# Tiles laid out anew in a partition: moved tiles at its lower end, weights, residual and scratch at its upper end

## The chip, the core and the metric

The kernel runs on one core of a Trainium2 chip. The metric is the time of one execution on the device in microseconds, the median of several. The on-chip memory that the engines work from (SBUF) has 128 partitions; a tile takes the same bytes in each of them, so its place is told by one number, its first byte in a partition. A matmul of TensorE has two operands in that memory: the stationary tile, 128 columns that are loaded into the array ahead of it (a weight load, PEld in the profile), and the moving tile, whose columns (up to 512) are streamed through. The profile names them as out<-moving,stationary.

## The reference

A sequence of 512 tokens of width 1024, in float32, goes through two layers of a first block and one of a second:

```
for l in range(2):
    x = x + 0.5 * swiglu_ffn(x, ffn1...)          # 1024 -> 2816 -> 1024
    h = rms_norm(x, mix_norm[l])
    aq, ak, av, bq, bk, bv, cq, ck, cv, cg, gates = split(h @ w_in[l])
    y_a, y_b, y_c = diff_attention(...), chunk_attention(...), retention(...)
    merged = sum over a, b, c of sigmoid(gates) * (y @ w_branch)
    x = x + merged @ w_out[l]
    x = x + 0.5 * swiglu_ffn(x, ffn2...)
h = rmsnorm(x, norm_mix)                          # second block
q, k, v, z, xbc, dt_raw, g_lru, x_lru = split(h @ w_in_2)
x = x + concat(dilated_attention, ssd_mixer, rglru_mixer) @ w_out_2
x = x + swiglu(rmsnorm(x, norm_ffn), ...)
out = rmsnorm(x, norm_final)
```

## The kernel before

**Numbers in two parts.** Every big product is made of three matmuls in a reduced float32 type (fp32r): both operands are split into a high and a low part (`split_late`: ScalarE writes the high one, VectorE the low one), and `mm3` issues high times high, low times high and high times low into one accumulator. Weights come from memory as a stream of units of 128x1024 (`load`, tile raw, on SyncE's queue), are split into wh and wl (`prepare`), three buffers each, and are used in the order of a fixed plan.

**Products.** Activations lie with features on partitions and the 512 tokens along the row. `fm_tile` makes 128 columns of h @ w: eight steps over k, the weights stationary, xgh[k] and xgl[k] (the normed input's two parts, one tile of 512 columns per k) moving; these are the gate and up products of the feed-forward layers and many of the mixers'. In `ffn` their results become yh and yl, eleven tiles of each for half of the 2816 features; the down products move these, eleven steps for each accumulator. In the mixers, `tm_products` (for q, k, v) is the other way round: xgh and xgl are stationary, and 384 or 512 columns of wh and wl move. The branches' outputs (y; those of branch A in the tiles of x) are moved by the branch products, mh and mb (the merged sum) by w_out, ys, yl and ya by the second block's w_out_2. Small products (scores, p @ v, transposes, sums over partitions) are taken up between the big ones, in an order that the program works out by its own estimates when it is traced. The first product of the second block, for dt, has eight stationary columns for each k, beside each other in one unit of weights.

**Where tiles lie.** Each pool (`Pool`, over a tile pool) is a stretch of the partition; tiles with one tag share its slots. In `Net.__init__` the pools are made one after the other from the lower end: constants; w (raw, wh, wl); x (the residual x in four pairs, xgh and xgl); s (scratch). On top of these come the pools of a stage, which are opened and closed with it: in `ffn` one with g, u, sg, yh and yl; in `mix` and `hybrid` y and mix. `x_pair` gives the memory of two tiles of x; while x is parked in memory, branch A's outputs use it.

The places as the built program has them, in bytes from the start of a partition, with the remainder by 256:

| tiles | before | rem. | after | rem. |
|---|---|---|---|---|
| wh, wl | 33,824 to 58,400 | 32 | 204,768 to 229,344 | 224 |
| x (four pairs) | 58,400 to 74,784 | 32 | 176,096 to 192,480 | 224 |
| xgh, xgl | 74,784 to 107,552 | 32 | 21,760 to 54,528 | 0 |
| diag (two) | 109,600 to 113,696 | 32 | 166,176 to 170,272 | 32 |
| yh, yl | 133,856 to 178,912 | 224 | 54,528 to 99,584 | 0 |
| y, ys, mh, mb | 123,616 to 229,088 | 224 | 54,528 to 164,096 | 0 |
| ones | 20,992 to 21,504 | 0 | the same | 0 |

Of the kernel before, what the change touches and what calls it, by code (L numbers as in the profile page):

```python
# [9 lines left out]
F32 = mybir.dt.float32  # L10
F32R = mybir.dt.float32r
# [5 lines left out]
P = 128  # L17
# [12 lines left out]
# columns of w_in  # L30
# [4 lines left out]
# columns of w_in_2  # L35
# [34 lines left out]
class Uses:  # L70
    """When the regions of a tile are written and read, by the estimate."""
# [17 lines left out]
class Model:  # L89
    """An estimate of when each instruction starts and ends; only the order of issue rests on it."""  # L90
# [4 lines left out]
    def tile(self, ring, bufs, name):  # L95
        """A new tile of a ring of slots."""
        slots = self.rings.setdefault(ring, [])
        if len(slots) < bufs:
            ready = 0.0
        else:  # L100
            old = slots.pop(0)
            ready = self.uses.pop(old).last()
            self.dead.add(old)
        slots.append(name)
        self.uses[name] = Uses(ready)
# [54 lines left out]
class Engine:  # L160
    """An engine's instructions, with an estimate of when each one ends."""
# [46 lines left out]
class Queue:  # L208
    """Transfers issued by an engine, in order."""
# [33 lines left out]
class Later:  # L243
    """The instructions of an engine for a generator: each is issued once it could soon start."""
# [17 lines left out]
class Thread:  # L262
    """A generator that yields the time at which to go on, or a condition."""
# [5 lines left out]
class Net:  # L269
    """Instructions are issued in the order in which they are traced here. The products with the big  # L270
    weights are traced by plain code; the chains of small steps of attention and the like are generators,
    taken up between those products when the estimate says that their operands are there."""
# [7 lines left out]
    def __init__(self, ctx, tc, io):  # L280
        self.tc, self.nc, self.io = tc, tc.nc, io
        self.now, self.last, self.threads, self.accs, self.current, self.seq = 0.0, 0.0, [], [], None, 0
        self.model, self.dma_free = Model(), 0.0
        self.v = Engine(self, self.nc.vector, "v")
        self.a = Engine(self, self.nc.scalar, "a")
        self.tv, self.ta = Later(self.v), Later(self.a)
        self.g = Queue(self, self.nc.gpsimd, "g")
        self.q = Queue(self, self.nc.sync, "q")
        self.aq = Queue(self, self.nc.scalar, "aq")
        self.plan = weight_plan()  # L290
        self.used, self.off, self.at, self.raws, self.splits = 0, 0, {}, [], []
        self.free = {k: [f"{k}_{i}" for i in range(n)] for k, n in self.LIMITS.items()}
        self.banks = set(range(self.BANKS))
        self.n = 0
        pool = lambda name, bufs, **k: self.pool(ctx, name, bufs, **k)
        self.const = pool("const", 1)
        self.wp = pool("w", 3)
        self.xp = pool("x", 1)
        self.sp = pool("s", 2)
        self.pp = pool("ps", 1, space=bass.MemoryType.PSUM)  # L300
        self.dram = pool("dram", 1, space=bass.MemoryType.DRAM)
# [13 lines left out]
    def ready(self):  # L315
        """The thread to go on with: of those that can, the oldest."""
        ok = [t for t in self.threads if (t.wake() if callable(t.wake) else t.wake <= self.now)]
        return min(ok, key=lambda t: t.rank) if ok else None
# [14 lines left out]
    def wait(self, cond):  # L333
        """For plain code."""
# [10 lines left out]
    def take(self, name):  # L345
        """For plain code: one of the slots of that name."""
        self.wait(lambda: self.free[name])
        return self.free[name].pop(0)

    def lock(self, name):  # L350
        """For generators."""
# [12 lines left out]
    def acc(self):  # L364
        """A bank for plain code; it is free when the generator given to evac is done."""
# [11 lines left out]
    def get_bank(self):  # L377
        """For generators: a bank of PSUM that nothing reads any more."""
# [13 lines left out]
    def main_bank(self):  # L392
        """For plain code."""
# [19 lines left out]
    def operands(self, out, ins):  # L413
        """For generators: waits until a product could start."""
# [25 lines left out]
    def load_consts(self):  # L440
# [11 lines left out]
        warm = c.tile([P, 1], F32, name="warm")  # L452
# [27 lines left out]
    def x_pair(self, j, dtype=F32):  # L480
        """The memory of two tiles of x."""
        t = self.xp.tile([P, 2, S], dtype, tag=f"x_{j}", name=self.nm("x"))
# [41 lines left out]
    def tiles(self, units):  # L524
        """128x128 stationary tiles in their order."""
# [24 lines left out]
    def token_rstd(self, sqs, count, eps, n=NT):  # L550
        """Squares [features, tokens] -> 1/rms as [tokens of a tile, tile]."""
# [10 lines left out]
    def spread(self, r, n=NT):  # L562
        """[tokens of a tile, tile] -> the same row of tokens on every partition, in a bank of PSUM: the column
        sums of diagonal blocks, in two parts."""
# [26 lines left out]
    def feed_norm(self, d, gain, feeds):  # L591
        """x[d] is final: its part of the next norm's input and of the sum of squares."""
# [44 lines left out]
    def fm_tile(self, name, l, c0):  # L637
        """128 columns of h @ w (before the norm's factor), features on partitions."""
# [5 lines left out]
    def tm_products(self, name, l, cols, evac):  # L644
        """Some columns of h @ w, tokens on partitions; evac(t, ps) for the tiles of tokens."""
# [16 lines left out]
    def tm_group(self, name, l, cols, nv):  # L662
        """q, k as [token, tile, 256] and v split, with the norm's factor."""
# [30 lines left out]
    def ffn(self, wg, wu, wd, l, factor, gain):  # L694
        self.end_norm()
        with ExitStack() as ctx:
            fp = self.pool(ctx, self.nm("ffn"), 2)
# [6 lines left out]
            def up(ps, got, y, before):  # L704
# [3 lines left out]
                y += [fp.tile([P, S], F32R, tag=t, name=self.nm(t), bufs=HALF) for t in ("yh", "yl")]  # L708
# [29 lines left out]
    def last_products(self, fp, wd, l, ys, factor):  # L738
        """The last products, the norm and the output for one half of the tokens, then for the other."""
# [61 lines left out]
    def rope(self, tm, cos, sin):  # L801
        """cos and sin: for the pairs of heads of q and of k; sin has its signs."""
# [13 lines left out]
    def to_fm(self, tm, c0, tag, scale=None):  # L816
        """128 columns of tm -> [column, token], split."""
# [17 lines left out]
    def scores(self, ps, q, k, i, c):  # L835
        """[query of tile i, key] of one member of the pair, keys up to tile i."""
# [5 lines left out]
    def new_p(self, i):  # L842
        """Probabilities of query tile i for both members, and columns for maxima, sums and their inverses."""
# [3 lines left out]
    def put_pT(self, pT, w, i, *before):  # L847
        """Row block i of a [query, key] matrix into the split [key, key tile, query]."""
# [14 lines left out]
    def new_pT(self):  # L863
        """The visible part of [key, key tile, query]: queries from the key tile's first one."""
# [5 lines left out]
    def av(self, v, pT):  # L870
        """[feature of v, query]"""
# [12 lines left out]
    def out_norm(self, b, o, gain, y, gate=None):  # L884
        """y = o / rms(o) * gain (* gate); o in bank b."""
# [17 lines left out]
    def setup_A(self, l):  # L903
        """-lambda, and cos and sin times the gains of q (with the scale of the scores) and of k."""
# [146 lines left out]
    def rel_rows(self, l, h):  # L1051
        """The biases of a pair of heads, by distance, once per partition."""
# [56 lines left out]
    def fill(self, l, kinds):  # L1109
        """Products for which there is always something to do: p parks tanh(gates / 2) of a tile of the branches  # L1110
        b and c, u parks two tiles of sigmoid(gates) * (y @ w) of branch a, doubled."""
# [43 lines left out]
    def silu_gate(self, l, h, out):  # L1155
        """2 silu(cg) of a head."""
# [13 lines left out]
    def merge(self, l, yb, yc, heads_c):  # L1170
        """sum over the branches of sigmoid(gates) * (y @ w), twice that before the split: the first loads, and a
        function that does the rest."""
# [143 lines left out]
    def softplus(self, v, n):  # L1316
        """max(v, 0) + log1p(exp(-|v|)); the logarithm as 2 atanh(e / (2 + e))."""
# [19 lines left out]
    def lru_scale(self):  # L1337
        """4 softplus(-lambda) and -8 softplus(-lambda)"""
# [11 lines left out]
    def tconv(self, x, out, w, b, j, nj):  # L1350
        """Causal convolution of four taps along the tokens."""
# [7 lines left out]
    def lru_gates(self, j, ps, out):  # L1359
        """The convolution, sigmoid r and sigmoid i times the convolution."""  # L1360
# [23 lines left out]
    def lru_scan(self, parts, scale):  # L1384
        """a = exp(-8 r softplus(-lambda)), and sqrt(1 - a^2) = sqrt(t) (1 + a) with t = tanh(-log(a) / 2)."""
# [68 lines left out]
    def ssd(self, big, xbc, before):  # L1454
        """The scan over chunks of 128 tokens; leaves [feature, token] of each pair of heads, with the skip."""
# [6 lines left out]
        # token-major x (times dt, and times the decay to the chunk's end) and B  # L1462
# [21 lines left out]
        # C B^T per chunk and group: [key, chunk, query]  # L1484
# [11 lines left out]
        # states before each chunk: [state, chunk - 1, head, feature]  # L1496
# [86 lines left out]
    def hybrid(self):  # L1583
        self.end_norm()
        parked = self.park_x()
        with ExitStack() as ctx:
# [5 lines left out]
            # state space: dt, x, B, C  # L1592
# [11 lines left out]
            # recurrence: input and gates  # L1604
# [160 lines left out]
def fm_units(name, l, c0):  # L1765
    """In one transfer, but for the first of all."""
# [194 lines left out]
```

## Time and profile before

| | |
|---|---|
| time, median of 3 runs | 3282.43 us (3281.28 to 3287.72) |
| span of the profiled execution | 3283.1 us |
| TensorE, matmuls | 3264.9 us busy, 15592 |
| TensorE, weight loads | 2721.6 us busy |
| VectorE | 1874.0 us busy |
| ScalarE | 1230.7 us busy |
| moved by DMA | 343.51 MB, 105 GB/s over the span |

The profile is of one execution. Busy time of a group is the union of its instructions' times; a matmul's duration includes its way through the array, so durations of matmuls that follow each other overlap, and their rate is read from their starts. The granted clock of TensorE (PEclk) is given as a share of full speed: 1.00 is 2.4 GHz, 0.50 is 1.2 GHz.

### The profile page before, as it was taken

What the parts mean: (1) busy time and instruction counts of PE and PEld (TensorE: products, weight loads), DVE (VectorE), ACT (ScalarE), POOL (GpSimd) and SP (SyncE); (2) the same over time, 40 slices, a digit from 0 to 9 for tenths busy, and PEclk for the clock granted to TensorE, in tenths of its full rate; (3) what the DMA queues carried; (4) which work ended last, traced back from release to release, by engine and by line L of the source; (5) the groups of instructions that cost most, each with busy time, mean ns of one, the idle gap of its engine ahead of it and who ended that gap; (6) DMA issues with size and microseconds to landing.
All of it is one profiled execution on the core that took longest, in us unless ns stands there. A gap on an engine that the chain in (4) does not pass through costs nothing.

```text
span 3283.1 us, 39855 instructions
## 1 busy us (share of the span) xinstructions
PE 3264.9 (99%) x15592; PEld 2721.6 (83%) x15592; DVE 1874.0 (57%) x3574; ACT 1230.7 (37%) x1996; POOL 111.4 (3%) x206
## 2 busy tenths in 40 slices
PE   9999999999999999999999999999999999999998
PEld 7888888988788888888888888888888788888888
DVE  5434577766754345434478775665344777564345
ACT  4223344653332233222344564333223355642223
POOL 0000000000100000000010000110000000000000
PEclk9999999999999999999999999999999999999999
DMA  4222433223522222222243322342223313222224
GB/s 142 96 97 96 130 107 117 91 83 117 165 95 96 96 96 90 100 95 95 93 137 113 108 84 87 132 151 90 97 97 106 111 66 103 84 86 100 90 98 147
DMA packets 106413, 343.51 MB, mean 105 GB/s; under 512 B 19680, under 2 KB 20864, under 8 KB 106224
## 3 DMA queue, kind: packets, MB, share of 16 engines
q1 hardware_dynamic: 83520, 289.04, 26.5%
q0 software_dynamic: 22704, 51.93, 4.8%
q8 instruction: 122, 2.00, 0.2%
q14 instruction: 67, 0.55, 0.1%
HBM read 319.88 MB, written 26.21 MB: 105 GB/s over the span
## 4 chain that ended last, share of the span: by engine, by line
PE 75%; issue 24%; DVE 1%; DMA 0%; ACT 0%; SPq 0%; POOL 0%; DVEq 0%; POOLq 0%
PE acc L404 66%; PE b L404 7%; PE b L433 2%; DMA rowsA<-in_rows_dram 0%; DMA raw<-in_wst_dram 0%; DVE o L203 0%; DVE rst L203 0%; DVE og L203 0%; DVE rsy L203 0%; SPq L224 0%; DVE mb L203 0%; DVE p L203 0%; DVE y L203 0%; DVE tabA L203 0%; ACT y L203 0%
## 5 line engine op out<-in xcount | busy, mean ns | idle before, releaser
L404 PE MATMUL acc<-xgh,wh 128*128 128x512 f32 x2432 | 959.8, 395 | 1.8 <-ACT xgh L203 1.8
L404 PE MATMUL acc<-xgh,wl 128*128 128x512 f32 x2432 | 950.2, 391 | 0.0
L404 PE MATMUL acc<-xgl,wh 128*128 128x512 f32 x2432 | 949.9, 391 | 0.4 <-DVE xgl L203 0.3
L203 DVE TENSOR_TENSOR wl<-raw,wh 128x1024 fp32r<-128x1024 f32 (+3 forms) x563 | 669.2, 1189 | 470.3 <-ACT wh L203 467.8
L203 ACT CAST wh<-raw 128x1024 fp32r<-128x1024 f32 (+3 forms) x563 | 573.9, 1020 | 872.7 <-issue 444.5
L404 PEld LDWEIGHTS acc<-xgh,wh 128*128 128x128 f32 x2432 | 458.7, 189 | 100.3 <-issue 3.5
L404 PEld LDWEIGHTS acc<-xgh,wl 128*128 128x128 f32 x2432 | 458.2, 188 | 96.6
L404 PEld LDWEIGHTS acc<-xgl,wh 128*128 128x128 f32 x2432 | 458.6, 189 | 94.7 <-DVE xgl L203 1.8
L404 PE MATMUL acc<-yl,wh 128*128 128x512 f32 (+1 forms) x1032 | 382.6, 376 | 0.0
L404 PE MATMUL acc<-yh,wh 128*128 128x512 f32 (+1 forms) x968 | 361.7, 374 | 0.0
L404 PE MATMUL acc<-yh,wl 128*128 128x512 f32 (+1 forms) x968 | 361.5, 373 | 0.0
L404 PE MATMUL acc<-wh,xgh 128*128 128x384 f32 (+1 forms) x672 | 246.9, 367 | 0.0
L404 PE MATMUL acc<-wh,xgl 128*128 128x384 f32 (+1 forms) x672 | 235.4, 350 | 0.0
L404 PE MATMUL acc<-wl,xgh 128*128 128x384 f32 (+1 forms) x672 | 234.9, 350 | 0.0
L203 ACT ACTIVATE sg<-g 128x512 f32<-128x512 f32 x110 | 69.6, 633 | 432.2 <-DVE g L203 432.0
L404 PEld LDWEIGHTS acc<-yl,wh 128*128 128x128 f32 x1032 | 192.4, 187 | 39.7 <-issue 0.5
L404 PEld LDWEIGHTS acc<-yh,wl 128*128 128x128 f32 x968 | 181.8, 188 | 36.6
L404 PEld LDWEIGHTS acc<-yh,wh 128*128 128x128 f32 x968 | 181.2, 187 | 36.6
L203 DVE TENSOR_TENSOR g<-acc,rbc 128x512 f32<-128x512 f32 x110 | 76.1, 691 | 234.9 <-PE acc L404 234.7
L203 DVE TENSOR_TENSOR u<-acc,rbc 128x512 f32<-128x512 f32 x110 | 76.0, 691 | 195.7 <-PE acc L404 195.7
L404 PEld LDWEIGHTS acc<-wh,xgh 128*128 128x128 f32 x672 | 126.9, 189 | 15.7 <-issue 7.4
L404 PEld LDWEIGHTS acc<-wl,xgh 128*128 128x128 f32 x672 | 126.9, 189 | 6.4
(276 smaller groups left out, 3370.7 us busy)
## 6 DMA issues: line engine op xcount, KB each, us to landing
raw<-in_wst_dram SPq DMA_DIRECT2D x496, 512.0 KB, 3.2
raw<-in_wst_dram SPq DMA_DIRECT2D x64, 384.0 KB, 3.4
gpark<-gl POOLq DMA_DIRECT2D x48, 256.0 KB, 3.9
mb<-gpark POOLq DMA_DIRECT2D x48, 256.0 KB, 3.8
xpark<-x POOLq DMA_DIRECT2D x24, 256.0 KB, 5.6
x<-xpark POOLq DMA_DIRECT2D x24, 256.0 KB, 4.8
relscr<-in_rel_dram POOLq DMA_DIRECT2D x8, 639.0 KB, 21.1
bias<-relscr POOLq DMA_DIRECT2D x16, 256.0 KB, 5.1
```

Source lines behind the costliest of these rows:

```text
L203: return f(*a, **k)
L404: self.nc.tensor.matmul(out, lhsT, rhs, start=start, stop=stop)
L433: self.nc.tensor.transpose(out, in_, ident)
```

## The change

Pools can be made from the lower end of the partition (the default) or from the upper end (side="right"). The change makes the pool of xgh and xgl directly after the constants; w, a new pool r for the residual x, and s go to the upper end. The last of the constants, a tile of one column, is given 56 columns more, so that what comes after it starts on a multiple of 256 bytes. In `ffn`, yh and yl get a pool of their own (ffny), made ahead of the one with g, u and sg, so that they come directly after xgl. Nothing is computed in another way; comments and docstrings are gone too, so that lines are shifted by one or two. The order of the instructions on TensorE, VectorE, GpSimd and the queues is the same in the built program, name by name, and so are their waits; on ScalarE six waits are added, at three places.

```diff
         self.const = pool("const", 1)
-        self.wp = pool("w", 3)
         self.xp = pool("x", 1)
-        self.sp = pool("s", 2)
+        self.wp = pool("w", 3, side="right")
+        self.rp = pool("r", 1, side="right")
+        self.sp = pool("s", 2, side="right")
...
-        warm = c.tile([P, 1], F32, name="warm")
+        warm = c.tile([P, 1 + 56], F32, name="warm")[:, 0:1]
...
     def x_pair(self, j, dtype=F32):
-        t = self.xp.tile([P, 2, S], dtype, tag=f"x_{j}", name=self.nm("x"))
+        t = self.rp.tile([P, 2, S], dtype, tag=f"x_{j}", name=self.nm("x"))
...
     def ffn(self, wg, wu, wd, l, factor, gain):
...
+            fy = self.pool(ctx, self.nm("ffny"), HALF)
             fp = self.pool(ctx, self.nm("ffn"), 2)
...
-                y += [fp.tile([P, S], F32R, tag=t, name=self.nm(t), bufs=HALF) for t in ("yh", "yl")]
+                y += [fy.tile([P, S], F32R, tag=t, name=self.nm(t)) for t in ("yh", "yl")]
```

## Rows read from the trace of the kernel before

**Rows 1.** Page, busy us of each engine (share of the span) and instructions.

```profile
PE 3264.9 (99%) x15592; PEld 2721.6 (83%) x15592; DVE 1874.0 (57%) x3574; ACT 1230.7 (37%) x1996; POOL 111.4 (3%) x206
```

**Rows 2.** TensorE's waits, whole run: total us, times, longest us.

```profile
PE b L404 <- DVE rsy L203: 2.4, 1, 2.4
PE acc L404 <- ACT y L203: 1.8, 2, 0.9
```

**Rows 3.** Tile xgh, 3100 to 3210 us: count, durations in ns, first and last start.

```profile
L404 PE MATMUL acc<-xgh,wh x158: 389/389/389, 3100.1 to 3206.9; 128*128 128x512 f32 x158
```

**Rows 4.** Tile yl, 145 to 204 us, a down stretch.

```profile
L404 PE MATMUL acc<-yl,wh x72: 394/394/394, 144.7 to 194.4; 128*128 128x512 f32 x72
```

**Rows 5.** Tile mb, 900 to 937 us, w_out.

```profile
L404 PE MATMUL acc<-mb,wh x39: 393/393/398, 900.0 to 926.6; 128*128 128x512 f32 x39
```

**Rows 6.** Windows: length, TensorE busy (instructions), granted clock, DMA share, GB/s.

```profile
11.70:16.30 4.60, 4.60 (x12) 0.50 1.03 413
```

**Rows 7.** Timeline, first weights: start us, us, what.

```profile
12.08 0.63 PE L404 MATMUL acc<-xgh,wh 128*128 128x512 f32 x1
...
15.92 0.63 PE L404 MATMUL acc<-xgh,wh 128*128 128x512 f32 x1
```

**Rows 8.** Groups by form: shape and count, busy us, mean ns, idle before.

```profile
L404 PE MATMUL acc<-xgh,wh 128*128 128x512 f32 x2432 | 959.8, 395 | 1.8 <-ACT xgh L203 1.8
...
L404 PE MATMUL acc<-yl,wh 128*128 128x512 f32 x856 | 333.1, 395 | 0.0
...
L404 PE MATMUL acc<-wh,xgh 128*128 128x384 f32 x512 | 181.4, 354 | 0.0
...
L404 PE MATMUL acc<-wh,xgh 128*128 128x512 f32 x160 | 65.5, 409 | 0.0
...
L404 PE MATMUL acc<-mh,wh 128*128 128x512 f32 x128 | 50.6, 396 | 0.0
...
L404 PE MATMUL acc<-yh,wh 128*128 128x256 f32 x176 | 49.7, 282 | 0.0
...
L404 PE MATMUL acc<-x,wh 128*128 128x512 f32 x128 | 41.6, 406 | 0.0
```

**Rows 9.** Timeline, branch A's product over x, three matmuls to the next start.

```profile
678.37 0.61 PE L404 MATMUL acc<-x,wh 128*128 128x512 f32 x2
...
679.05 2.03 PE L404 MATMUL b<-pT,v 128*128 128x512 f32 x12
```

**Rows 10.** Timeline, a q, k, v product, twelve matmuls between these starts.

```profile
473.08 0.33 PE L404 MATMUL acc<-wh,xgh 128*128 128x384 f32 x1
...
475.16 0.33 PE L404 MATMUL acc<-wh,xgh 128*128 128x384 f32 x1
```

**Rows 11.** Tile yl, 3225 to 3229 us, the last down products.

```profile
L404 PE MATMUL acc<-yl,wh x12: 281/281/281, 3225.0 to 3228.9; 128*128 128x256 f32 x12
```

**Rows 12.** Timeline, product for dt: matmuls 1, 7 and the next after 18.

```profile
2575.24 0.39 PE L404 MATMUL b<-xgh,wh 128*8 128x512 f32 x1
...
2576.60 0.40 PE L404 MATMUL b<-xgh,wh 128*8 128x512 f32 x1
...
2579.39 0.95 PE L404 MATMUL b<-ones,sq 128*128 128x1 f32 x8
```

**Rows 13.** Timeline, switch from yl, yh to xgh: matmuls 1, 7 and 10.

```profile
194.86 0.39 PE L404 MATMUL acc<-xgh,wh 128*128 128x512 f32 x1
...
196.24 0.39 PE L404 MATMUL acc<-xgh,wh 128*128 128x512 f32 x1
...
196.92 0.39 PE L404 MATMUL acc<-xgh,wh 128*128 128x512 f32 x1
```

**Rows 14.** Timeline, a matmul over diag between those over xgh.

```profile
31.91 0.40 PE L404 MATMUL acc<-xgh,wl 128*128 128x512 f32 x1
32.15 0.39 PE L404 MATMUL b<-diag,ones 128*128 128x512 f32 x1
32.38 0.39 PE L404 MATMUL acc<-xgh,wh 128*128 128x512 f32 x1
```

## Prediction

> **What bounds the kernel now.** I read the page's busy table first: TensorE is busy 3264.9 of 3283.1 us, every other engine far less [rows 1]. Then the waits of TensorE: the longest of them all comes to 2.4 us in total [rows 2]. So nothing feeds TensorE late, and what an edit is worth is read from how fast TensorE itself goes, that is from the time between the starts of two matmuls that follow each other. The "busy" and "mean ns" columns of the groups don't tell that, since durations overlap (395 ns a matmul, at less than 240 ns from start to start); the view of one tile does, which gives the first and the last start of a group.
>
> In a gate and up stretch every third matmul is xgh,wh: 158 of them start between 3100.1 and 3206.9 us [rows 3], so one matmul takes 106.8/157/3 = 0.2268 us. In a down stretch 72 of yl,wh start between 144.7 and 194.4 us [rows 4]: 49.7/71/3 = 0.2333 us. The shape is the same, 128x512, the clock granted is full, and only the tile moved is another one. w_out, which moves mb and mh, has 26.6/38/3 = 0.2333 us too [rows 5]. What would be free of any stall the trace tells as well: early on, the granted clock is 0.50 [rows 6], and from the start at 12.08 to that at 15.92 us there are nine matmuls, 0.4267 us each [rows 7]. 512 columns at 1.2 GHz are 0.4267 us, one column a cycle and nothing else; at 2.4 GHz that is 0.2133 us. So at full clock the gate and up products lose 13.4 ns a matmul and the down products 20.0 ns. This loss is all that a new layout can touch: 7296 matmuls of the first kind (three groups of 2432) and 3432 of the second (2376 in the down products; y 480, ys 96, the yl of the recurrence 96, mh and mb 384) [rows 8], 98 and 69 us.
>
> **What the change does, part by part.** By the program as built, the instructions of TensorE, VectorE, GpSimd and the queues stand in the same order with the same waits, and ScalarE has six waits more. I cost those at nothing: the most that TensorE waits for one tile of ScalarE's is 1.8 us over the whole run [rows 2], ScalarE being done ahead nearly always; without that cover six waits would cost some tenths of a microsecond. What moves is addresses, in bytes from the start of a partition:
>
> 1. xgh and xgl: 74,784 to 107,552, each 32 past a multiple of 256, go to 21,760 to 54,528, on multiples of 256.
> 2. yh and yl: 133,856 to 178,912, 224 past a multiple, go to 54,528 to 99,584, on multiples.
> 3. y, ys, mh, mb: 123,616 to 227,040, 224 past; 3072 of the 3432 matmuls (with part 2) end below 107,600, 152 between there and 123,600, 208 above.
> 4. wh and wl: 33,824 to 58,400, 32 past, go to 204,768 to 229,344, 224 past. They are stationary nearly everywhere, but the q, k, v products move them: 1536 matmuls of 384 columns and 480 of 512 [rows 8]. So the rule "what is moved lies low" isn't kept for these.
> 5. x: 58,400 to 74,784 goes to 176,096 to 192,480, 224 past. Branch A's products move it (192 matmuls).
>
> What rate an address gets is the whole question. In before, moved tiles between 33 and 108 thousand bytes (wh, x, xgh) have the fast rate: three matmuls over x take 680 ns [rows 9], and those over wh with 384 columns 2.08/12 = 0.1733 us, 13.3 above their 0.1600 [rows 10]. All from 123 thousand up have the slow one. But the same split is one of 32 against 224 past a multiple of 256. Either way of reading it, parts 2 and 3 gain and 4 and 5 lose, and part 1 stays at 0.2268; that is the sum I take:
>
> - 3072 x (233.3 - 226.8) = -20.0 us. The 152 in the band that before doesn't show: 0 to -1.0, I take -0.5.
> - x and the moved weights of 512 columns: 0, if a place that high were no slower, to 672 x 6.5 = +4.4 us, which I take.
> - The weights of 384 columns: bounds 0 (the loss doesn't depend on the place) and 20 ns of loss as with 512 columns, 1536 x 6.7 = +10.3. I take the slow rate per column, 384/512 x 233.3 = 175.0, so 1536 x 1.7 = +2.6, since the 256-column products over yl, at 3.9/11/3 = 0.1182 us [rows 11], lose 11.5 ns of 106.7 and not 20: the slow loss goes by columns.
> - These 528 matmuls of 256 columns: at the fast rate per column 0.1134, 0 to -2.5; I take -1.0, as they may hang on the weight load.
>
> Sum: -20.0 - 0.5 + 4.4 + 2.6 - 1.0 = -14.5 us; ends -20.0 - 1.0 - 2.5 = -23.5 and -20.0 + 4.4 + 10.3 = -5.3. The profiled execution's span is 3283.1 us, 0.7 above the median of 3282.43, so I start from the median: 3268, 3259 to 3277.
>
> Other engines: VectorE and ScalarE are at 57% and 37% [rows 1], and a slower or faster access of theirs is hidden as long as TensorE's waits stay at a few microseconds.
>
> **The rivals.**
>
> *A. The start on a multiple of 256 takes more of the loss away* (no moved tile of a full-rate matmul starts on one before, so no row excludes it). The losses read so far are 13.4 and 20.0 ns, a step of 6.6 apart. One step less for all: 7296 x 6.6 + 3432 x 13.2 = 93, less 7 for parts 4 and 5: 3196. The whole of it, down to 213.3: 98 + 69 + 6 - 7 = 166: 3116. For it: what is lost differs between 32 and 224, so the offset may be what counts, and 0 is the natural best. Against: 32 and 224 touch as many rows of 256 bytes, and nothing shows that 0 is better than 32.
>
> [...]
>
> *B. The stall hangs on how the moved and the stationary tile lie to each other, and the new pairing is a bad one.* In before the fast pairs (xgh with wh, wh with xgh, x with wh) are all alike modulo 256; y with wh is 192 off. The place where this shows is the product for dt: xgh is moved as always, but its stationary slices have 8 columns and start 32 bytes further each time. The first six matmuls take 1.36 us, 226.7 ns each; the next twelve 2.79 us, 232.5 ns each [rows 12], with xgh where it always is. After the same switch from y to xgh with ordinary weights, six matmuls take 1.38 us and the rate is fast from then on [rows 13]. And a matmul over diag, 32 past at 109,600, with ones on a multiple of 256, makes two matmuls 0.47 us instead of 0.453 [rows 14]. After the change all of xgh and y lie 32 off their weights, and over 100,000 bytes away from them as well. If that costs what dt's twelve show, xgh gets 7296 x 5.7 = +42 us, y -3, part 4 up to +2: 3323. At the slow rate for all: +48 + 2.6 + 3 = 3336. The mean of dt's 18, 230.6 ns, would give 3302. Against it: dt also differs by its short weight load. This is the case on the other side, and it decides from 229.6 ns on: there the gate and up products lose the 20 us that the down products can gain at most.
>
> *C. Nothing moves.* The two rates could belong to the products and not to the addresses, for instance to the lengths of the sums (8 and 11 tiles): 3282. Against it: the products of branch A and those of b and c have the same code and length, and x is fast where y isn't [rows 8, 9].
>
> [...]
>
> **How the numbers follow.** The forecast, low or better offset gives 226.8 ns: 0.37. A: 0.21. B: 0.26. C: 0.14. Something else, on either side: 0.02. The predicted time is the forecast's, 3268, with its own range of 3259 to 3277. As A and B are on opposite sides, the range reaches to the one-step end of A, 3196, and to B's slow rate, 3336; left out are the deeper part of A (some 0.13) and what lies beyond B (0.04). About 0.2% (6.6 us) is what a measurement of this kernel can tell from no change. Faster: most of the forecast (its end near 3277 falls inside the 0.2%) and A, 0.57. Same: C and that end, 0.15. Slower: B and the rest, 0.28.
>
> **What would show it.** In the profile after, the first and last start of xgh,wh in a gate stretch, and of yl,wh in a down stretch, three matmuls apart. Forecast: 0.2268 and 0.2268. A: 0.220 or less for both. B: 0.230 or more for xgh, and y no better than 0.232. C: 0.2268 and 0.2333. The q, k, v products of 384 columns go from 0.1733 to 0.175, or stay. Waits of TensorE stay at a few microseconds; were they tens, the sum would be wrong in its ground, as it would be if a stretch showed a clock under 1.00 that before didn't have. Wrong, too, is the sum if the two rates come down unequally, since then place and offset both count.

## The result, and the profile after

The changed kernel is slower: 3325.69 us (median of 4 runs, 3323.54 to 3327.55) against 3281.86 us for the kernel before, a ratio of 1.0129 with a 95% interval of 1.0117 to 1.0141. The profiled execution has a span of 3325.7 us, 42.6 more than the one of before.

The engines' busy line on the page after, to be set beside [rows 1]:

```profile
PE 3308.8 (99%) x15592; PEld 2719.5 (82%) x15592; DVE 1874.0 (56%) x3574; ACT 1230.6 (37%) x1996; POOL 111.9 (3%) x206
```

TensorE has 43.9 us more of busy time with the same instructions; VectorE, ScalarE and GpSimd have what they had. TensorE's longest waits in total (engine, line, what it waited for: total us, times, longest) are as before, the two of [rows 2] and the one for xgh, which came to 1.8 us then too; the matmuls' line is L405 now:

```profile
PE b L405 <- DVE rsy L203: 2.4, 1, 2.4
PE acc L405 <- ACT xgh L203: 1.8, 2, 1.2
PE acc L405 <- ACT y L203: 1.8, 2, 0.9
```

So TensorE has no new wait and no late operand. Nor is it the clock: the mean granted clock of the profiled execution is 0.996 before and 0.997 after. What changed is the time from one matmul's start to the next, as the views of single tiles show (count, durations in ns, first and last start in us): a gate and up stretch, a down stretch, a stretch of w_out, and the last down products of 256 columns.

```profile
L405 PE MATMUL acc<-xgh,wh x119: 393/396/397, 3127.4 to 3210.0; 128*128 128x512 f32 x119
...
L405 PE MATMUL acc<-yl,wh x61: 393/396/397, 155.1 to 197.1; 128*128 128x512 f32 x61
...
L405 PE MATMUL acc<-mb,wh x53: 393/396/397, 900.1 to 936.5; 128*128 128x512 f32 x53
...
L405 PE MATMUL acc<-yl,wh x18: 277/279/280, 3265.8 to 3271.7; 128*128 128x256 f32 x18
```

Every third matmul is of the form shown. xgh: 82.6/118/3 = 0.2333 us, where [rows 3] give 0.2268. yl: 42.0/60/3 = 0.2333, mb: 36.4/52/3 = 0.2333, both as in [rows 4, 5]. The 256 columns: 5.9/17/3 = 0.1157 with starts to 0.1 us, 0.1167 with starts to the nanosecond, where [rows 11] give 0.118. The durations say it too: a matmul over xgh is recorded with 389 ns before and with 393 to 397 after, the values that y has.

Adding up, in both traces, the times from each matmul's start to the next by the kind of matmul gives where the 42.6 us are (us):

```
moved tile, columns                 count   before    after   change
xgh and xgl, 512                     7296   1679.3   1720.5    +41.2
yh and yl, 512                       2472    577.9    577.9      0.0
y, ys, mh, mb, 512                    960    228.7    228.6     -0.1
moved weights, 512                    480    114.4    117.5     +3.1
moved weights, 384                   1536    282.0    281.0     -1.0
yh and yl, 256                        528     62.4     61.9     -0.5
x, 512                                192     46.4     46.6     +0.2
all of TensorE                              3274.7   3317.2    +42.5
```

The gate and up products and the others over xgh lost their fast rate, and y did not get it. Of the 7296 matmuls over xgh, 6473 took 226 to 228.5 ns before; after, 66 do. These 6473 lose 43.3 us. The other 823 had no fast rate to lose and give 2.2 us back: 694 of them are among the first twelve after a matmul of another kind, since a series that begins so can take about ten matmuls to reach its fast rate even with operands that lie alike (as at 444 us, where nine intervals of 224 to 236 ns come ahead of the steady 227), and 113 are the last before one. This is why the sum is 41 us and not 7296 x 6.6 = 48.

### The profile page after: what moved, and what is told of

It reads as the page before. It is cut to its first block, busy times and chain, and to the rows that moved or that the text cites. A ratio compares the mean times of both kernels' runs of the same rounds, so it can differ in the third digit from the quotient of the medians.

```text
span 3325.7 us, 39859 instructions
## 1 busy us (share of the span) xinstructions
PE 3308.8 (99%) x15592; PEld 2719.5 (82%) x15592; DVE 1874.0 (56%) x3574; ACT 1230.6 (37%) x1996; POOL 111.9 (3%) x206
## 4 chain that ended last, share of the span: by engine, by line
PE 98%; DVE 1%; DMA 0%; ACT 0%; issue 0%; SPq 0%; DVEq 0%
PE acc L405 90%; PE b L405 7%; PE b L434 2%; DMA x<-in_xT_dram 0%; DMA rowsA<-in_rows_dram 0%; ACT xgh L203 0%; DVE o L203 0%; DVE og L203 0%; SPq L224 0%; DVE rst L203 0%; DVE mb L203 0%; DVE rsy L203 0%; ACT sq L203 0%; DVE p L203 0%; DVE y L203 0%
## 5 line engine op out<-in xcount | busy, mean ns | idle before, releaser
L405 PE MATMUL acc<-xgh,wh 128*128 128x512 f32 x2432 | 971.9, 400 | 1.8 <-ACT xgh L203 1.8
L405 PE MATMUL acc<-xgl,wh 128*128 128x512 f32 x2432 | 963.0, 396 | 0.0
L405 PE MATMUL acc<-xgh,wl 128*128 128x512 f32 x2432 | 962.6, 396 | 0.1
L405 PEld LDWEIGHTS acc<-xgh,wh 128*128 128x128 f32 x2432 | 457.8, 188 | 114.5 <-issue 3.4
L405 PEld LDWEIGHTS acc<-xgh,wl 128*128 128x128 f32 x2432 | 457.2, 188 | 112.0 <-DVE wl L203 0.5
L405 PEld LDWEIGHTS acc<-xgl,wh 128*128 128x128 f32 x2432 | 457.7, 188 | 109.1 <-DVE xgl L203 1.4
L405 PE MATMUL acc<-yl,wh 128*128 128x512 f32 (+1 forms) x1032 | 383.0, 376 | 0.0
L405 PE MATMUL acc<-yh,wh 128*128 128x512 f32 (+1 forms) x968 | 362.2, 374 | 0.0
L405 PE MATMUL acc<-yh,wl 128*128 128x512 f32 (+1 forms) x968 | 361.9, 374 | 0.0
L405 PE MATMUL acc<-wh,xgh 128*128 128x384 f32 (+1 forms) x672 | 248.9, 370 | 0.0
L405 PE MATMUL acc<-wh,xgl 128*128 128x384 f32 (+1 forms) x672 | 236.7, 352 | 0.0
L405 PE MATMUL acc<-wl,xgh 128*128 128x384 f32 (+1 forms) x672 | 236.6, 352 | 0.0
L405 PEld LDWEIGHTS acc<-yl,wh 128*128 128x128 f32 x1032 | 192.7, 188 | 39.3 <-issue 0.5
L405 PEld LDWEIGHTS acc<-yh,wl 128*128 128x128 f32 x968 | 181.5, 188 | 36.4
L405 PEld LDWEIGHTS acc<-yh,wh 128*128 128x128 f32 x968 | 181.5, 188 | 36.3
L405 PEld LDWEIGHTS acc<-wh,xgh 128*128 128x128 f32 x672 | 127.3, 189 | 16.3 <-issue 7.3
L405 PEld LDWEIGHTS acc<-wl,xgh 128*128 128x128 f32 x672 | 127.4, 190 | 6.9
```

The lines of the kernel that those rows point to most:

```text
L405: self.nc.tensor.matmul(out, lhsT, rhs, start=start, stop=stop)
```

## The experiments

The theories at this point. **Pairing** (the prediction's rival B; theory 1 in the expectations below): the rate depends on the distance between the starts of the stationary and the moved tile, modulo 256. Before, wh and xgh have distance 0, wh and y 64 (32 less 224, plus 256); after the change both have 224. **Place** (what the forecast rested on, in one reading; theory 2): the rate depends on where in the partition the tiles lie. **Own offset** (its other reading, and rival A; theory 3): it depends on the moved tile's own start modulo 256. In what follows the distance is always the start of the stationary tile less that of the moved one, modulo 256; the prediction counts the other way round, so its 192 and 32 are 64 and 224 here.

**The pairs alone (pair_map).** Sections of 48 matmuls on one large tile:

```
+ps = pp.tile([P, S], F32, tag="acc", name=name)
+for g in range(2):
+    for k in range(8):
+        hi, lo = at(s0 + ds * k, P), at(s0 + ds * (24 + k), P)
+        mh, ml = at(m0 + 2 * dm * k, S), at(m0 + dm * (2 * k + 1), S)
+        nc.tensor.matmul(ps, hi, mh, start=k == 0, stop=False)
+        nc.tensor.matmul(ps, hi, ml, start=False, stop=False)
+        nc.tensor.matmul(ps, lo, mh, start=False, stop=k == 7)
```

> Only a series of matmuls of 128x512, on nothing but copies of one part of the input; the products of the reference are left out. Each section is 48 matmuls in the order of the gate and up products (high weights with high and low part of the input, low weights with the high part, eight tiles on), with given addresses of the moved and the stationary tiles. Theory 1 (pairing): what counts is the distance of the moved from the stationary tile modulo 256; the eight sections in which both lie alike take 226.7 ns a matmul, those 64 and 192 bytes apart 233.3, and the far sections (moved tiles from 20,736 to 196,608, weights at 20,736 or 204,800) show the same by their distance modulo 256 alone. Theory 2 (place): all 64 near sections take 226.7, and the far ones 233. Theory 3 (the moved tile's own offset): all sections with the moved tile 32 past take 226.7 whatever the weights' place, those at 0 and 224 take 233.

The names in the rows give the moved and the stationary start modulo 256 and the region: "near" has the moved tiles from 73,728 and the weights from 33,792; "ohigh" 20,736 and 204,800, nearly the places of the changed kernel; "thigh" 163,840 and 204,800. Tile views, first and last start of every third matmul, so 45 matmuls lie between:

```profile
L61 PE MATMUL m000s000near<-big x16: 389/389/389, 34.7 to 44.9; 128*128 128x512 f32 x16
...
L61 PE MATMUL m000s224near<-big x16: 393/396/397, 112.6 to 123.1; 128*128 128x512 f32 x16
...
L61 PE MATMUL m224s032near<-big x16: 393/396/398, 669.4 to 679.9; 128*128 128x512 f32 x16
...
L61 PE MATMUL m032s032ohigh<-big x16: 389/389/397, 747.3 to 757.5; 128*128 128x512 f32 x16
...
L61 PE MATMUL m000s224ohigh<-big x16: 392/394/397, 780.6 to 791.1; 128*128 128x512 f32 x16
...
L61 PE MATMUL m032s032thigh<-big x16: 389/389/389, 1069.5 to 1079.7; 128*128 128x512 f32 x16
```

10.2/45 = 0.2267 us where both lie alike, whatever the offset and the region; 10.5/45 = 0.2333 for the pair of the changed kernel (m000s224) and for y's pair of before (m224s032). With the starts at a nanosecond's resolution, the mean of the last 36 intervals of each section, over all 64 near sections by their distance (8 sections each):

```
distance     0      32     64     96     128         160    192    224
ns           226.7  233.3  233.3  234.3  232.3-233.3 233.3  228.9  233.3
```

Two sections of the same distance differ by less than 0.3 ns but at 128, and the 36 far sections, at the distances 0, 32, 64 and 224, have the values of the near ones within 0.1 ns. Sections that move one tile over and over, or keep one stationary place, have them too: 226.7 alike and 233.3 at 64. So neither the place nor the moved tile's own offset counts, and a start on a multiple of 256 is worth nothing by itself.

Which matmul's stationary tile counts can be read where one distance follows another. In the kernel before, the interval from the last matmul over xgh to the first over yh is 226 or 227 ns at all nine such switches, though that next matmul's own operands are 64 off; its weights are alike with xgh. At the seven borders of this map where a pair that lies alike is followed by a stationary tile 32 on, the moved tile's place unchanged, the interval is 235 ns. So an interval runs slow, as far as these switches show, when the stationary tile of the next matmul is off from the tile being moved; its weight load falls in that interval (in the kernel before, between matmuls over xgh, xgl, yh and yl, nine in ten loads start 2 to 4 ns after the matmul ahead does; they take 187 or 188 ns). The other way round, where a stationary tile alike with the moved one follows a pair at 224, it is 226 or 227 ns in six of eight cases, 232 and 234 in two. Inside a section, and inside the kernel's stretches, both stationary tiles have the same distance.

**y brought into line, high as it was (before_y32).**

```
+        self.sp.tile([P, 16], F32, tag="gap", name="gap", bufs=1)
```

> The kernel before with 64 bytes more in the pool below the y tiles: y, ys, yh, yl, mh and mb lie 32 past a multiple of 256 like the weights, as high as before. Theories 1 and 3: y goes to 226.8 ns, 3432 x 6.5 ns = -22 us, so 3260. Theory 2: 3282, y at 233.3.

Measured 3263.39 us, ratio 0.9935 (0.992 to 0.995). Tile views of yl in a down stretch, mb in w_out and xgh in a gate stretch:

```profile
L404 PE MATMUL acc<-yl,wh x60: 389/389/389, 149.7 to 189.8; 128*128 128x512 f32 x60
...
L404 PE MATMUL acc<-mb,wh x39: 389/389/389, 900.2 to 926.1; 128*128 128x512 f32 x39
...
L404 PE MATMUL acc<-xgh,wh x89: 389/389/389, 3120.0 to 3179.8; 128*128 128x512 f32 x89
```

yl: 40.1/59/3 = 0.2266; mb: 25.9/38/3 = 0.2272; xgh: 59.8/88/3 = 0.2265. Sixty-four bytes, and 3258 of the 3432 matmuls over y take 226 to 228.5 ns, at addresses up to 229 thousand; 5 did before. Place falls.

**The changed kernel with all at 224 (after_all224).**

```
-        warm = c.tile([P, 1 + 56], F32, name="warm")[:, 0:1]
+        warm = c.tile([P, 1 + 48], F32, name="warm")[:, 0:1]
```

> The changed kernel with its pad 32 bytes smaller: xgh and y lie 224 past a multiple of 256, as wh, wl and x do at the other end of the partition. Theory 1: all pairs lie alike, 226.8 ns for xgh and y, 3326 - 10,728 x 6.6 ns = -71, so 3255 to 3260. Theory 2: nothing moves, 3326. Theory 3: 224 is a slow offset, 3326 or more.

Measured 3261.66 us, ratio to the kernel before 0.9933 (0.9916 to 0.9949): 64 us less than the changed kernel, by a pad that is 32 bytes smaller.

```profile
L405 PE MATMUL acc<-yl,wh x59: 389/389/389, 149.9 to 189.4; 128*128 128x512 f32 x59
...
L405 PE MATMUL acc<-xgh,wl x89: 389/389/389, 3120.0 to 3179.9; 128*128 128x512 f32 x89
```

39.5/58/3 = 0.2270 and 59.9/88/3 = 0.2269. All places are those of the change, but for 32 bytes; the weights are 150 thousand bytes away from xgh. The own offset falls as well: 224, y's offset when it was slow, is fast here.

**The pad in the kernel before (before_x0).**

```
-        warm = c.tile([P, 1], F32, name="warm")
+        warm = c.tile([P, 1 + 56], F32, name="warm")[:, 0:1]
```

> The kernel before with the 224 bytes of pad that the change has: wh, x and xgh on multiples of 256, y 192 past. Theories 1 and 2: xgh with wh lie alike and near as before, y stays 192 off its weights: 3282. Theory 3: xgh gets the rate that it has on a multiple of 256 in the changed kernel, 233.4 ns, 7296 x 6.6 = +48, so 3330.

Measured 3280.24 us, ratio 0.9991 (0.9982 to 1.0). xgh on a multiple of 256 is fast here, because its weights are on one too:

```profile
L404 PE MATMUL acc<-xgh,wh x89: 389/389/389, 3120.1 to 3179.9; 128*128 128x512 f32 x89
...
L404 PE MATMUL acc<-yl,wh x58: 394/394/394, 150.0 to 189.9; 128*128 128x512 f32 x58
```

59.8/88/3 = 0.2265, and y, 64 off as before, 39.9/57/3 = 0.2333.

**The change without its move of the weights (after_wleft).**

```
-        self.wp = pool("w", 3, side="right")
+        self.wp = pool("w", 3)
```

> The change without its move of the weights: wh and wl lie low, behind xgh, on a multiple of 256 like xgh and y; residual and scratch stay at the top, y stays low. Pairing: xgh and y at 226.8, some 65 us less than the changed kernel as in the run with all at 224, and x now 32 off (192 x 6.6 = +1): 3262. If instead the low y or the start on a multiple of 256 costs something by itself, it stays between 3290 and 3326.

Measured 3264.94 us (3256.91 to 3270.46), ratio 0.9948 (0.9931 to 0.9965).

```profile
L405 PE MATMUL acc<-yl,wh x60: 389/389/389, 149.8 to 190.0; 128*128 128x512 f32 x60
...
L405 PE MATMUL acc<-xgh,wh x85: 389/389/389, 3120.2 to 3177.3; 128*128 128x512 f32 x85
```

0.2271 and 0.2266. So of all that the change does, the loss comes with one part: the weights went to the other end and came to lie 224 past a multiple of 256 there, while the tiles at the low end were padded to a multiple. This version, after_all224 and before_y32 lie some 20 us below the kernel before; their own differences are within their spread.

**The change without its pad (after_nopad).**

```
-        warm = c.tile([P, 1 + 56], F32, name="warm")[:, 0:1]
+        warm = c.tile([P, 1], F32, name="warm")
```

> The changed kernel without its pad of 224 bytes: xgh and y lie 32 past a multiple of 256, wh stays 224 past, so the weights lie 192 on from the moved tiles. Pairing, with the first map's 228.9 ns at 192: 10,728 x (233.3 - 228.9) = 47 us less than the changed kernel, 3279, that is the kernel before again. Place in the partition: 3326. The moved tile's own offset: 32 was the fast one, 226.8, so 3255.

Measured 3311.81 us, ratio 1.0085 (1.007 to 1.01): a miss by all three. The tile views show why: xgh and yl in the first feed-forward stretch, then in the second.

```profile
L405 PE MATMUL acc<-xgh,wh x103: 392/392/392, 59.7 to 129.7; 128*128 128x512 f32 x103
...
L405 PE MATMUL acc<-yl,wh x59: 394/394/395, 149.9 to 189.7; 128*128 128x512 f32 x59
...
L405 PE MATMUL acc<-xgh,wh x100: 397/397/398, 960.0 to 1029.3; 128*128 128x512 f32 x100
...
L405 PE MATMUL acc<-yl,wh x72: 397/397/398, 1059.6 to 1109.3; 128*128 128x512 f32 x72
```

70.0/102/3 = 0.2288 and 39.8/58/3 = 0.2287 first, 69.3/99/3 = 0.2333 and 49.7/71/3 = 0.2333 later, with the same tiles at the same addresses. The distance of 192 has two rates; the first held through the whole of the first feed-forward part, some 340 us, the second through the whole of the next, some 360 us, each without a break. So most of the 47 us that the first map's 228.9 promised did not come.

**What the entry does (entry_map).** The sections of the first map, with one matmul of 256 to 300 columns ahead:

```
+            nc.tensor.matmul(ps[:, :n], at(33792, P), at(73728, n), start=True, stop=True)
             for k in range(8):
```

> Only a series of matmuls as in the maps before; the products of the reference are left out. Twelve distances, and each entered twelve times: one matmul of 256, 260 ... 300 columns, lying alike, stands ahead of 24 matmuls of 512 columns at the distance, so that they begin at another moment against whatever they run into. It is about the two rates of the changed kernel without its pad, 228.9 ns in its first stretch and 233.3 in most of the others at the same distance of 192. Theory 1c (one rate to a distance): all twelve entries of 192 end at 228.9, and what makes the kernel's other stretches slow is no matter of the pairs. Theory 1d (a rate is a pattern that the series falls into, by how it begins): 192 shows both 228.9 and 233.3 among its entries, some other distances show two rates too, and 0 shows 226.7 from every entry.

Timeline, start and duration in us, of two sections at distance 192, entered after 256 and after 276 columns; twelve matmuls lie between the rows of each:

```profile
515.35 0.39 PE L47 MATMUL d192e256x<-big 128*128 128x512 f32 x1
...
518.10 0.39 PE L47 MATMUL d192e256x<-big 128*128 128x512 f32 x1
...
543.51 0.40 PE L47 MATMUL d192e276x<-big 128*128 128x512 f32 x1
...
546.31 0.40 PE L47 MATMUL d192e276x<-big 128*128 128x512 f32 x1
```

2.75/12 = 0.2292 and 2.80/12 = 0.2333. Rates over twelve matmuls near each section's end, twelve entries a distance (left out are 96, with 234.2 to 234.6, and 128, with 232.5 to 233.3):

```
distance   0        32       64       120      160      212      224      192             252             228
ns         226.7    233.3    233.3    226.7    233.3    236.7    233.3    228.9, 1: 233.3 233.3, 4: 226.7 231, 1: 226.7
```

Theory 1d has the rates: 192, 228 and 252 show two each, 228.9 and 233.3 at 192, chosen by how the series begins. Distance 0 shows 226.7 from all twelve entries, and 224, that of the changed kernel, 233.3 from all twelve. This is how after_nopad can have both; what set each of its stretches on its rate was not followed up.

**Widths and finer distances (width_map).**

```
+    for d in range(0, 256, 4):
+        out.append((f"w512d{d:03d}x", 33792 + d, 512, P))
+    for w in (128, 256, 384):
+        for d in range(0, 256, 32):
+            out.append((f"w{w}d{d:03d}x", 33792 + d, w, P))
```

> Only a series of matmuls as in the first map, with the moved tiles on multiples of 256; the products of the reference are left out. Sections: the stationary tile 0, 4, 8 ... 252 past, 512 columns moved; moved tiles of 128, 256 and 384 columns at eight distances; distances of 256, 768, 1024 and 1280; stationary tiles of 8, 32 and 64 columns at distances 0, 32 and 192. Theory 1a: the loss of a pair that lies alike is one fixed price for each matmul, 13.4 ns: 384 columns 173.4, 256 columns 120.1, and 8 stationary columns 226.7 as well; the distance counts modulo 256 only, so 256, 768, 1024 and 1280 give 226.7; no distance goes under 226.7. [...]

Tile views, 45 matmuls between the first and the last start: 384 and 256 moved columns at distances 0 and 32; 8, 32 and 64 stationary columns at 0; a distance of 256; and the slowest but one of the 64 distances:

```profile
L56 PE MATMUL w384d000x<-big x16: 334/334/338, 836.0 to 843.8; 128*128 128x384 f32 x16
...
L56 PE MATMUL w384d032x<-big x16: 336/336/336, 844.3 to 852.1; 128*128 128x384 f32 x16
...
L56 PE MATMUL w256d000x<-big x16: 281/283/334, 790.5 to 795.9; 128*128 128x256 f32 x16
...
L56 PE MATMUL w256d032x<-big x16: 277/280/286, 796.3 to 801.6; 128*128 128x256 f32 x16
...
L56 PE MATMUL w512d000c08x<-big x16: 389/389/389, 946.8 to 957.0; 128*8 128x512 f32 x16
...
L56 PE MATMUL w512d000c32x<-big x16: 391/394/397, 979.8 to 990.3; 128*32 128x512 f32 x16
...
L56 PE MATMUL w512d000c64x<-big x16: 387/390/393, 1013.5 to 1023.9; 128*64 128x512 f32 x16
...
L56 PE MATMUL w512d0256far<-big x16: 389/389/402, 903.2 to 913.5; 128*128 128x512 f32 x16
...
L56 PE MATMUL w512d212x<-big x16: 397/397/402, 625.4 to 636.1; 128*128 128x512 f32 x16
```

384 columns: 7.8/45 = 0.1733 at both distances. 256 columns: 5.4/45 = 0.1200 at 0 and 5.3/45 = 0.1178 at 32; they are better off out of line. Eight stationary columns: 10.2/45 = 0.2267, as with 128. But 32 and 64 columns have no fast rate although they lie alike: 10.5/45 = 0.2333 and 10.4/45 = 0.2311, over the last 36 intervals 231.7 and 230.0 ns; 32 columns at a distance of 32 take 240.0, and 64 columns are better at 192, with 228.3, than alike. No theory here had foreseen it, and no run tells the reason. Distance 256: over the last 36 intervals 226.7 ns, and the same at 768, 1024 and 1280. Distance 212: 10.7/45 = 0.2378, its entry counted. For 128 and 8 stationary columns theory 1a has it. A matmul without loss is put here at half of the 426.7 ns that 512 columns take at a granted clock of 0.50 [rows 6, 7], and at 384 and 256 columns in proportion, an estimate; against it, alike, the loss over the last 36 intervals is 13.3 ns of 213.3 with 512 moved columns, 13.3 of 160.0 with 384 and 13.3 of 106.7 with 256, one price for each matmul at these three widths. Of the 64 distances none goes under 226.7; seven reach it (0, 120, 132, 144, 156, 228, 252). Of these entry_map has 0 and 120 fast from every entry, 228 from one of twelve and 252 from four; 132, 144 and 156 were tried in one section each.

## Why the prediction was wrong

**The bound: right.** TensorE without waits, and a loss that stands in the time from start to start. The six further waits of ScalarE cost nothing that shows; TensorE's waits are as before, none over 2.4 us.

**Part 1, xgh "stays at 0.2268": this is the step that failed.** It was costed at 0 and is +41.2 us. The prediction took the rate of an address from the two groups of [rows 3, 4] and read it as a matter of where the moved tile lies, alone. That reading leaves out the other operand. Of its two forms, moreover, only the one by place has rows near xgh's new start: no full-rate moved tile lay on a multiple of 256 before, as the prediction itself says under A, so by the other form the 0.2268 was assumed and not read. With the pairs, the same rows are distances of 0 and 64, and the change makes both 224: xgh at 233.3 by the first map.

**Parts 2 and 3, y: -20.5 us forecast, -0.1 measured** (0.0 and -0.1 in the table). y left one slow distance (64) for another (224). The price of 6.5 ns a matmul was right: before_y32, which brings the distance to 0, shows 21.8 us less over the 3432.

**Parts 4 and 5.** Moved weights of 512 columns and x: +4.4 forecast, +3.1 and +0.2 measured; moved weights come from 0 to 32, and x from 0 to 0 with its weights, as both went to the same end together. So its share of the term had no cause. The weights of 384 columns: +2.6 forecast, -1.0 measured; the map has 173.3 both at 0 and at 32. The 256 columns: -1.0 forecast, -0.5 measured. The scaling by columns, which both terms rested on, is not how it goes: in width_map the loss is 13.3 ns alike at 256, 384 and 512 columns, and at a distance of 32 it is 11.1, 13.3 and 20.0.

**Rival B was the case**, with 3323 us from the price of dt's twelve matmuls, 232.5 ns [rows 12]; it had xgh at +42 (measured +41.2), y at -3 (0). Its point of decision, 229.6 ns for xgh, was passed with 233.3. That its +42 comes so near is in part luck: it put 5.7 ns on all 7296 matmuls, where 6473 lost 6.7 ns each and the others lost nothing. The time lies inside the stated range of 3196 to 3336 through this rival alone; the sum's own 3259 to 3277 had the wrong sign. The row that carried B was one of two places in the rows of the kernel before where one moved tile, at one place, met stationary tiles of different starts; it separates the readings, and the rates of xgh, y, x and the moved weights agree with each. The row is even stronger than it was read: of its first six matmuls only three lie alike (680 ns together), and the next three, 32 off, take 687; with starts to the nanosecond the six have 227.8 ns each, not 226.7. It was set aside because dt's weights have 8 columns, but width_map has eight columns at distance 0 with 0.2267 and at 32 with 231 ns: the distance does it there too. The other place, a matmul over diag with ones 224 on, points the same way, with 0.47 us for two intervals [rows 14].

**Rival A falls.** On a multiple of 256, xgh takes 0.2265 us with weights alike (before_x0) and 0.2333 with weights at 224. At the best of the 64 distances of width_map, all with the moved tiles on multiples of 256, a matmul takes 226.7 ns, 13.3 more than the 213.3 of [rows 6, 7].

**Rival C falls** with before_y32, where the same products change their rate, y from 0.2333 us to 0.2266. In pair_map a shift of one operand by 32 bytes makes 226.7 ns into 233.3, so for these matmuls the two operands' addresses are not independent.

What inside TensorE makes the rate go by the distance, what the fixed 13.3 ns are, and what picks one of two rates at a distance such as 192, no run here tells.

## What to carry to other kernels

Where TensorE is the bound, read the time from start to start by kinds of matmul, and for each kind write down the starts of both operands modulo 256: in fp32r with 512 moved and 128 stationary columns, laying stationary and moved tiles alike was worth 6.6 ns of 233.3. For other shapes it has to be measured: with 256 moved columns (117.8 ns at 32, 120.0 alike), or with 64 stationary ones (228.3 at 192, 230.0 alike), another distance was faster. Aligning one side to a round number was worth nothing here and broke a pairing that was there by chance, as one pool grew from the other end of the memory: xgh, put on multiples of 256 with its weights 224 past, went from 226.8 ns to 233.3. When two readings explain all rows but one, weigh that one row by what it separates, not by how few its matmuls are.

## What was not expected of the hardware

- With 512 moved and 128 stationary columns the rate goes by the distance modulo 256 and by nothing else of the addresses that was tried: 36 sections at nine pairs of regions and four distances agree with the near ones within 0.1 ns.
- Some distances have two steady rates, chosen by how the series begins, which then held for 340 us and more in the kernel: 228.9 or 233.3 ns at 192.
- Steps of 4 bytes matter: 226.7 ns at distance 120, 231.7 at 124, 236.7 at 212.
- By the switches in pair_map and in the kernel before it is the stationary tile of the next matmul that has to match the tile being moved: 235 ns where it lies 32 on, 226 or 227 where it lies alike.
- Alike is not best for every stationary tile: 231.7 ns with 32 columns and 230.0 with 64, against 226.7 with 8 and with 128.
- Matmuls of 128 moved columns take 111.6 to 111.7 ns at all eight distances tried; those of 256 columns are slower alike (120.0) than at 96 (117.3).
